# A hybrid layer on one core: attention's first pair of heads built in place beside the values' projection, and the MLP's first pass in a fixed order

## The chip, the cores and the metric

The kernel runs on one core of one Trainium2 chip. The time is the device time of one execution in microseconds (us); lower is better. All times are of float32 inputs of fixed shape (one sequence of 1024 tokens, width 1024).

## What is computed

The reference, cut to what matters here:

```python
h = rms(x) * (1 + scale_m) + shift_m            # scales, shifts, gates: silu(c) @ w_ada + b_ada
proj = h @ w_in                                 # (1024, 4104): fox q,k,v,gate,forget + retention q,k,v,gate
fox = forgetting_attention(rms(fq)*qg, rms(fk)*kg, fv, log_sigmoid(f_logit + b))   # 8 heads of 64
ret = retention(rope(rq), rope(rk), rv)                                            # 4 heads of 128
x = x + gate_m * (concat(rms(fox)*.. , rms(ret)*..) @ w_out)
h = rms(x) * (1 + scale_f) + shift_f
u = square(relu(h @ w_mlp_in))                  # (1024, 4096)
x = x + gate_f * (u @ w_mlp_out)
```

Forgetting attention is causal softmax attention whose logits also take a difference of cumulated forget gates, cum[t] - cum[s].

## The kernel before

**Precision.** Every large product is made of three TensorE matmuls: both operands are split into a rounded part and a remainder (split_w: ScalarE casts, L138, VectorE subtracts, L139), and hi·hi, hi·lo and lo·hi are added up in PSUM. A matmul is 128 rows by 512 columns.

**Stages, in order of time.** Conditioning and norm; the input projections (proj_group, one call for 512 output columns and half the tokens: 8 steps k of 12 matmuls, L295 to L297); the retention chunks, hooked in between; attention over four pairs of heads; the output projection (L937 and after); the second norm; the MLP.

**Attention.** The last projection is that of the values (fv), in two halves. Between them, prep_pair(0) makes the first pair of heads ready: four parts (fk and fq, two halves of the tokens each) transpose four blocks on TensorE (L641), cast and subtract (L644 to L649) into scratch (fkH, part of kl, and for fq the tile wh), and then 11 copies by DMA bring each head's two 64-row halves to the places that the scores want (L656 to L660). Only then is wh free for what it is named for, the cumulated gates of each head over 128 partitions (L662, 512 KB each), because the same tile was the scratch of fq. The second half of fv runs interleaved with the first scores S (L707, L708); VectorE adds the gates and takes the row maximum from PSUM (L711), ScalarE takes exponentials (L723), TensorE transposes p (L743) and multiplies by v (L752). Other pairs are prepared beside the pair ahead of them.

**The MLP's first pass.** It is a Strassen-like scheme in eight "Eighths" e0 to e7, of 512 columns of w_mlp_in each. One Eighth has seven products of 24 matmuls: in order one, two, six, five, seven, three, four. Its weights are four blocks of 512 KB named 11, 21, 12, 22 (load, L1090); products use blocks or differences of them ("tees", L1144 and L1147, 2 = 22 - (12 - 11); six, L1156 and L1157; the difference 2 has a tile named wt). Before a product its block is split (halve) into one of two shared buffers (mr), so the split of one product can run while the one before it multiplies, and no earlier. Results are squared (L1115 to L1118) and u is written to HBM (put, L1122). For e0 and e1 the first products stand in a block written by hand (manual_schedule: TensorE, ScalarE and VectorE follow the program's order), in which the last four token blocks of the second norm are transposed (h2_turn) and combined (make_s2) between the products.

**The gates of the MLP.** w_mlp_out is multiplied by gate_f on GpSimd before the second pass: 32 blocks n, each loaded (gate_load, 512 KB), multiplied in two halves and, for every other pair, subtracted (gate_times, L1201 and L1203), and stored (gate_store, two of 256 KB). There are two buffers. They are hung on the steps of the first pass (52 steps: ten of e0 and e1, then seven per Eighth): n is loaded at step 2 + 3·(n // 2) + n % 2, so two per three steps.

**The MLP's second pass.** Four quarters of seven products of 48 matmuls (L1304) over blocks a.. (of u) and b.., t1 (of the gated weights) that are loaded from HBM (L1275); the first difference on GpSimd is wdt = b22 - t1 (t_two, L1330).

**What sets the order.** A scheduler orders each engine's instructions from a simulated timeline, except in blocks written by hand and for single instructions kept in program order (the gates' DMAs). Nearly all DMAs are issued by one engine, SP, in its order, and an issue that waits holds up those behind it.

The split, and the loop by which the sides are hung on the steps before:

```python
    for n in range(32):
        at = 2 + n // 2 * 3 + n % 2
        for d, what in ((0, gate_load), (1, gate_times), (2, gate_store)):
            side[at + d].append(lambda what=what, n=n: what(n))
```

Of the kernel before, what the change touches and what calls it, by code (L numbers as in the profile page):

```python
# [19 lines left out]
P = 128  # L20
S = 1024
# [28 lines left out]
def tile_block(  # L50
# [573 lines left out]
    def prep_pair(pr):  # L624
# [6 lines left out]
        def part(name, half):  # L631
# [6 lines left out]
            hd, rest = split[name]  # L638
            tp = (xbank if pr else rbank)(f"{name}p{pr}{half}")
            for i in range(4):  # L640
# [24 lines left out]

    proj_group("fv", 2 * FW, 0, evac_fox("fv"), ret_hook(1))
    while todo:
        ada_hook(0)
    for n, m in enumerate((2, 5)):
# [4 lines left out]
        Q.dma_start(rows_d[n, :].rearrange("(k p) -> k p", p=P), gs)  # L674
    for _ in ret:
        pass
    ops, parts = prep_pair(0)
    for part in parts:
# [295 lines left out]
    def h2_norm(t):  # L974

        xt = x2_tok(t)
        rr = r_x[:, t : t + 1]
        A.activation(ra([P, D], f"x2sq{t}"), xt, AF.Square, accum_out=rr)
        V.tensor_scalar(rr, rr, 1.0 / D, EPS, op0=ALU.mult, op1=ALU.add)
        rsqrt_(rr, 1)  # L980
        xn = [t2([P, CH], f"xn{t}{n}") for n in range(2)] if t < 5 else None
# [89 lines left out]
    W2 = 2 * P  # L1071

    class Eighth:
        def __init__(self, e):
# [4 lines left out]
        def load(self, names):  # L1079
            for name, make in (("11", raw), ("21", f4), ("12", f4), ("22", f4)):  # L1080
                if name in names:
                    r, c_ = int(name[0]) - 1, int(name[1]) - 1
                    if self.e == 1 and name == "22":
                        both = s8([P, 2, 4, W2], "wu1_22")
                        self.b["2"], w = both[:, 0], both[:, 1]
# [4 lines left out]
                    Q.dma_start(w, wup_v[:, 4 * r : 4 * r + 4, at : at + W2])  # L1090

        def halve(self, name):
            s = self.split[name] = mr([P, 2, 4, W2], f"wu{self.e}s{name}", F32R)
            split_w(self.b[name], s[:, 0], s[:, 1])

# [24 lines left out]
        def put(self, n, st):  # L1120
            at = self.e % 2 * 2 * CH
            Q.dma_start(u_d[self.e // 2][n][:, at : at + 2 * CH], st.rearrange("p f c -> p (f c)"))  # L1122

# [8 lines left out]
        def two(self):  # L1132
            Y = [self.make[2 + f](f"Y{self.e}_{f}") for f in range(2)]
            self.product("A12", "21", Y, True)
            if self.e > 1:
                self.tees()
            for f in range(2):
                V.tensor_tensor(self.c11[:, f], Y[f], self.c11[:, f], op=ALU.add)
                self.square(self.c11, f)
            self.put(0, self.c11)  # L1140

        def tees(self):
            b = self.b
            V.tensor_tensor(b["12"], b["12"], b["11"], op=ALU.subtract)  # L1144
            if self.e != 1:
                b["2"] = ra([P, 4, W2], f"wt{self.e}")
            V.tensor_tensor(b["2"], b["22"], b["12"], op=ALU.subtract)  # L1147

        def six(self):
# [5 lines left out]
            b = self.b  # L1155
            V.tensor_tensor(b["11"], b["2"], b["11"], op=ALU.subtract)  # L1156
            V.tensor_tensor(b["21"], b["21"], b["2"], op=ALU.subtract)  # L1157

# [31 lines left out]
    def gate_load(n):  # L1190
        if not gf:
            for hf in range(2):
                gf.append(r2([P, CH], f"gf{hf}"))
                Q.dma_start(gf[hf], rows_d[1, hf * CH : (hf + 1) * CH].partition_broadcast(P))
            wg.append(s8([P, 2, 2, CH], "wg"))
        tc.keep_in_program_order(Q.dma_start(wg[0][:, n % 2].rearrange("p h c -> p (h c)"), wdn_v[:, n, :]))

    def gate_times(n):
        w = wg[0][:, n % 2]
        for hf in range(2):  # L1200
            G.tensor_tensor(w[:, hf], w[:, hf], gf[hf], op=ALU.mult)  # L1201
        if n % 4 < 2:
            G.tensor_tensor(w[:, 1], w[:, 1], w[:, 0], op=ALU.subtract)  # L1203

    def gate_store(n):
        e, c_, f = n // 4, n // 2 % 2, n % 2
        at = (e % 2 * 2 + f) * CH
        for hf in range(2):
            tc.keep_in_program_order(Q.dma_start(wd_d[e // 2][2 * c_ + hf][:, at : at + CH], wg[0][:, n % 2, hf]))

# [28 lines left out]
    with tc.manual_schedule(engines={ENG.PE, ENG.Activation, ENG.DVE}):  # L1239
        for n, t in enumerate(HI):  # L1240
            if n == 0:
                e0.one()
            elif n == 1:
                e0.two()
            else:
                e1.one()
            h2_turn(t, xn[t])
            make_s2(t)
            if n == 0:
                e0.tees()  # L1250
# [13 lines left out]
    for what in sum(side[len(steps) :], []):  # L1264
        what()

    x2b = []
    for q in range(4):
# [46 lines left out]

        for name in ("a11", "b11", "a12", "b21"):
            load(name)
        X = [lower[i](f"V{q}_{i}") for i in range(4)]
        product(1, blk["a11"], two("b11"), X, True, 0)
        if q == 0:  # L1320
            for n in range(4):
                x2b.append(s8([P, 2, D], f"x2b{n}"))
                Q.dma_start(x2b[n].rearrange("p i d -> p (i d)"), x2_d[n])
        for name in ("s1", "t1", "b22"):
            load(name)
        add(X, 0, 0)
        V.tensor_tensor(blk["a11"], blk["s1"], blk["a11"], op=ALU.subtract)  # L1327
        t_two = [raw([P, 2, CH], f"wdt{q}{g}") for g in range(2)]
        for g in range(2):
            G.tensor_tensor(t_two[g], two("b22")(g), two("t1")(g), op=ALU.subtract)  # L1330
# [6 lines left out]
        load("a22")  # L1337
        product(6, blk["a11"], lambda g: t_two[g], X, False, 0)
        add(X, 0, 1)
# [59 lines left out]
```

## Time and profile before

| what | value |
|---|---|
| three runs | 1384.39, 1377.92, 1380.03 us, median 1380.03 |
| the profiled execution | 1383.38 us, of which the span of the trace is 1381.6 |
| granted TensorE clock, mean of the span | 0.975 |
| TensorE busy | 1288.2 us, 93% of the span |
| VectorE, ScalarE, GpSimd busy | 974.7, 515.8, 460.4 us |

Times in the trace count from the start of its span. The table of engines says how long each had an instruction in flight; it doesn't say who waited for whom. In a timeline a row has start, length, engine, line, operation, the written and the read tiles, the shape, how many are put together (x24), and in brackets the idle time before it and what ended it.

### The profile page before, as it was taken

How to read it: one execution, taken by the hardware profiler on the slowest of the kernel's cores; microseconds unless marked ns; L12 is line 12 of the kernel's file. 1: busy time of each engine (PE TensorE's matmuls, PEld its weight loads, DVE VectorE, ACT ScalarE, POOL GpSimd, SP SyncE). 2: the span in 40 equal slices, each digit the busy share in tenths (PEclk: the TensorE clock that was granted, in tenths of full speed). 3: DMA queues.
4: the chain of work that ended last, by engine and by line, in shares of the span. 5: the costliest groups of instructions: out<-in, count | busy, mean ns of one | idle time of the engine just before them, and what ended most of it. 6: DMA issues, size and time to landing. Idle time of an engine off the chain costs nothing. (4 is left out here: it accounts for less than half of the span.)

```text
span 1381.6 us, 16679 instructions
## 1 busy us (share of the span) xinstructions
PE 1288.2 (93%) x6131; PEld 1042.5 (75%) x6131; DVE 974.7 (71%) x1486; ACT 515.8 (37%) x801; POOL 460.4 (33%) x364
## 2 busy tenths in 40 slices
PE   5899899999999899999976898889999899999998
PEld 3678777888888666678864786678888778888887
DVE  6758897476754367753687574668867989888883
ACT  3642212343333366652544432222334242424240
POOL 1129451156622013322340034644553714050500
PEclk9899999999999999999997999999999999999999
DMA  9656566534357574832550348667669450514202
GB/s 292 187 126 164 151 171 141 132 100 139 115 168 174 140 166 116 291 138 78 181 168 16 107 160 263 218 221 234 234 208 354 179 215 29 199 46 152 92 31 92
DMA packets 123601, 220.51 MB, mean 160 GB/s; under 512 B 9896, under 2 KB 70376, under 8 KB 117888
## 3 DMA queue, kind: packets, MB, share of 16 engines
q1 hardware_dynamic: 100640, 202.68, 47.8%
q10 hardware_dynamic: 22880, 16.78, 3.9%
q8 instruction: 48, 0.79, 0.2%
q14 instruction: 33, 0.27, 0.1%
HBM read 159.55 MB, written 48.34 MB: 150 GB/s over the span
## 5 line engine op out<-in xcount | busy, mean ns | idle before, releaser
L1304 PE MATMUL V<-sb,sa 128*128 128x512 f32 x768 | 180.3, 392 | 6.0 <-DVE sb L139 4.7
L1201 POOL TENSOR_TENSOR wg<-wg,gf 128x512 f32<-128x512 f32 x64 | 107.5, 1703 | 223.1 <-DMA wg<-in_w_mlp_out_dram 120.0
L1304 PEld LDWEIGHTS V<-sb,sa 128*128 128x128 f32 x768 | 145.1, 189 | 37.8 <-DVE sb L139 5.9
L135 POOL TENSOR_TENSOR sm<-sm 128x8 f32<-128x8 f32 (+2 forms) x48 | 62.0, 1298 | 138.5 <-DVE sm L253 48.8
L1304 PE MATMUL U<-sb,sa 128*128 128x512 f32 x384 | 88.8, 389 | 0.0
L1304 PEld LDWEIGHTS U<-sb,sa 128*128 128x128 f32 x384 | 72.1, 188 | 14.9
L138 ACT CAST sb<-b 128x1024 fp32r<-128x1024 f32 x40 | 40.7, 1052 | 103.5 <-PE V L1304 57.5
L238 DVE SCALAR_TENSOR_TENSOR wa<-wa,sm 128x128 f32<-128x128 f32 (+1 forms) x154 | 72.4, 470 | 3.3
L1330 POOL TENSOR_TENSOR wdt<-b,t 128x1024 f32<-128x1024 f32 x8 | 24.3, 3060 | 136.9 <-DMA b<-wd_d 136.9
L1282 DVE TENSOR_TENSOR x2b<-V,x2b 128x512 f32<-128x512 f32 x64 | 42.5, 683 | 35.0 <-PE V L1304 35.0
L711 DVE CUSTOM_DVE_ANT_0 p<-S,wh 128x512 f32<-128x512 f32 (+3 forms) x96 | 49.9, 552 | 24.1 <-DMA wh<-nc_d 16.2
L139 DVE TENSOR_TENSOR sa<-a,sa 128x2048 fp32r<-128x2048 f32 x20 | 60.3, 3015 | 4.2 <-ACT sa L138 4.1
L139 DVE TENSOR_TENSOR sb<-b,sb 128x1024 fp32r<-128x1024 f32 x40 | 55.4, 1410 | 3.5 <-ACT sb L138 1.6
L701 POOL TENSOR_SCALAR_AFFINE_SELECT wh<-wh 128x128 f32<-128x128 f32 x64 | 18.2, 293 | 108.2 <-DVE sm L711 53.1
L723 ACT ACTIVATE p<-p,sm 128x1024 f32<-128x1024 f32 (+7 forms) x64 | 49.1, 770 | 4.4 <-DVE sm L719 3.7
L707 PE MATMUL S<-kt,qt 128*128 128x512 f32 (+3 forms) x96 | 38.7, 408 | 9.2 <-DVE sm L711 6.6
L138 ACT CAST sa<-a 128x2048 fp32r<-128x2048 f32 x20 | 38.2, 1911 | 22.3 <-DVE a L1327 11.0
L1304 PE MATMUL W<-sb,sa 128*128 128x512 f32 x192 | 45.1, 389 | 0.0
L743 PE MATMUL pt<-ident,p 128*128 128x128 f32 x288 | 40.6, 282 | 2.6 <-ACT p L723 2.6
L743 PEld LDWEIGHTS pt<-ident,p 128*128 128x128 f32 x288 | 31.7, 142 | 13.4 <-issue 8.1
L1304 PEld LDWEIGHTS W<-sb,sa 128*128 128x128 f32 x192 | 36.1, 188 | 7.5
L752 PE MATMUL av<-pT,fv 128*64 128x256 f32 (+1 forms) x320 | 40.2, 373 | 0.0
(391 smaller groups left out, 3449.3 us busy)
## 6 DMA issues: line engine op xcount, KB each, us to landing
wu<-in_w_mlp_in_dram SPq DMA_DIRECT2D x32, 512.0 KB, 4.5
wg<-in_w_mlp_out_dram SPq DMA_DIRECT2D x32, 512.0 KB, 4.8
wd_d<-wg SPq DMA_DIRECT2D x64, 256.0 KB, 3.6
a<-u_d SPq DMA_DIRECT2D x12, 1024.0 KB, 6.4
b<-wd_d SPq DMA_DIRECT2D x12, 1024.0 KB, 7.1
wa<-in_w_ada_dram ACTq DMA_DIRECT2D x10, 1024.0 KB, 5.7
wam<-in_w_ada_dram SPq DMA_DIRECT2D x16, 512.0 KB, 7.7
u_d<-ua SPq DMA_DIRECT2D x16, 512.0 KB, 3.0
```

Of the source, the lines that this page charges most:

```text
L135: G.tensor_tensor(ap, ap, mhalf.to_broadcast([P, n]), op=ALU.pow)
L138: A.copy(h_ap, raw_ap)
L139: eng.tensor_tensor(l_ap, raw_ap, f32(h_ap), op=ALU.subtract)
L238: V.scalar_tensor_tensor(w[:, 0], w[:, j], c_act[:, j : j + 1], w[:, 0], op0=ALU.mult, op1=ALU.add)
L707: T.matmul(sp[n], qt[:, n, dg], kt[:, n, c_], start=True, stop=False)
L711: V.tensor_tensor_reduce(ps[n][:, c_], sp[n], wh[:, n, c_], -1.0, 3.4e38, op0=ALU.add, op1=ALU.min, accum_out=mcs[n][c0 // CH])
L723: A.activation(ps[n][:, :W], ps[n][:, :W], AF.Exp, bias=mcs[n][0], scale=-1.0, accum_out=den[:, 2 * i + n : 2 * i + n + 1],)
L743: T.transpose(tp[:, n, i * P : (i + 1) * P], ps[i][n][:, j * P : (j + 1) * P], ident)
L752: T.matmul(av[own, at], fox_pair_of("fv", pr)[:, j, n * FD : (n + 1) * FD], pts[j][:, n, i0 * P :], start=(j == 0), stop=(j == 2 * gg + 1),)
L1201: G.tensor_tensor(w[:, hf], w[:, hf], gf[hf], op=ALU.mult)
L1282: V.tensor_tensor(xs, banks[i], xs, op=ALU.add)
L1304: T.matmul(banks[i], sa[pa][:, a, ii], sb[pb_][a // 2][:, a % 2, :], start=(first and a == 0 and m == 0), stop=(a == 3 and m == 2), skip_g ...
```

## The change

1. **Attention.** The first pair gets a function of its own, first_pair. ScalarE and VectorE write each head's own 64 partitions straight into kt, kl and qt, two operations of 64 partitions where one of 128 stood (four more on each of the two engines), the remainder of q goes to a tile of its own (fqL), the two loads of the gates go out first, and 6 copies by DMA are left of 11. The four parts are called at k = 2, 4, 6 of the first half of fv and right after it.
2. **The second norm** of five token blocks uses other buffers (r2 for t2), which leaves t2 to the gates' gf.
3. **The hand-written block.** e1's block 11 is split right behind e0's tees, e1's 21 ahead of e1's first product, e0's difference 2 behind e1's second product; adding and squaring c11 of e0 and e1 leaves the block. e1's 22 and 2 become two half tiles each.
4. **The first pass.** SP follows the program's order through all steps. Stores of u go out one step later, behind that step's sides. The gates have four buffers and are loaded at step 12 + n, one per step, each in two DMAs.
5. **The second pass.** The first loads are a11, b11, t1, b22, a12, b21; t_two comes ahead of the first product; of the four x2b loads two stand behind product 1 and two behind a22.

The core of the diff:

```diff
+    def first_pair(pr):
+        klt, kt, qt, wh = (s8([P, 2, S], f"{name}{pr}", dt) for name, dt in (("kl", F32R), ("kt", F32R), ("qt", F32R), ("wh", F32)))
+        for n in range(2):
+            Q.dma_start(wh[:, n, :], nc_d[2 * pr + n, :].partition_broadcast(P))
...
+            if name == "fk":
+                for n, (own, _) in enumerate(ROWS):
+                    A.copy(kt[own, n, hs], tp[own, :])
+                for n, (own, _) in enumerate(ROWS):
+                    V.tensor_tensor(klt[own, n, hs], tp[own, :], f32(kt[own, n, hs]), op=ALU.subtract)
...
+    def prep_hook(k):
+        ada_hook(k)
+        if k == 0:
+            ops, made = first_pair(0)
+            parts.extend(made)
+        elif k % 2 == 0:
+            parts.pop(0)()
-    proj_group("fv", 2 * FW, 0, evac_fox("fv"), ret_hook(1))
+    proj_group("fv", 2 * FW, 0, evac_fox("fv"), prep_hook)
...
-        at = 2 + n // 2 * 3 + n % 2
+        at = 12 + n
...
+        e0.one()
+        h2_turn(HI[0], xn[HI[0]])
+        make_s2(HI[0])
+        e0.tees()
+        e1.halve("11")
+        e0.two()
+        h2_turn(HI[1], xn[HI[1]])
+        make_s2(HI[1])
+        e1.halve("21")
+        e1.one()
+        h2_turn(HI[2], xn[HI[2]])
+        make_s2(HI[2])
         e1.two()
+        e0.halve("2")
     e1.tees()
+    e0.end_two()
     split_part("S1", "r21", whole)
+    e1.end_two()
...
-    for n, step in enumerate(steps):
-        step()
-        for what in side[n]:
+    with tc.manual_schedule(engines={ENG.SP}):
+        for n, step in enumerate(steps):
+            due = list(stores)
+            stores.clear()
+            step()
+            for what in side[n] + due:
...
-        for name in ("a11", "b11", "a12", "b21"):
+        for name in ("a11", "b11", "t1", "b22", "a12", "b21"):
             load(name)
```

**What moves on TensorE, in the second half of fv.** Before, the first scores come behind the fifth step (ws_fv_4):

```order
L297 MATMUL pp_fv_3669<-ws_fv_4_3766,hT_355 128x512
L295 MATMUL pp_fv_3673<-ws_fv_4_3766,hT_355 128x512
L296 MATMUL pp_fv_3673<-ws_fv_4_3766,hT_355 128x512
L297 MATMUL pp_fv_3673<-ws_fv_4_3766,hT_355 128x512
L707 MATMUL S_3683<-kt_3602,qt_3603 128x512
L708 MATMUL S_3683<-kl_3601,qt_3603 128x512
L295 MATMUL pp_fv_3661<-ws_fv_5_3793,hT_397 128x512
```

and with the change inside the third step (ws_fv_2) of the last token block, two heads close together:

```order
L296 MATMUL pp_fv_3676<-ws_fv_1_3694,hT_223 128x512
L297 MATMUL pp_fv_3676<-ws_fv_1_3694,hT_223 128x512
L295 MATMUL pp_fv_3676<-ws_fv_2_3723,hT_269 128x512
L757 MATMUL S_3686<-kt_3434,qt_3435 128x512
L758 MATMUL S_3686<-kl_3433,qt_3435 128x512
L296 MATMUL pp_fv_3676<-ws_fv_2_3723,hT_269 128x512
L757 MATMUL S_3687<-kt_3434,qt_3435 128x512
L758 MATMUL S_3687<-kl_3433,qt_3435 128x512
```

The six score tiles of 512 columns (two matmuls each) now all stand inside the second half; before, the last two came behind its last matmul. Three of the four groups of transposes (L641, now L676) moved from the second half of fv into the first.

**What moves on ScalarE, in the hand-written block.** ua is the tile of c11 and c22, h2S that of the combined second-norm rows, wu1s that of e1's split. Before, the cast of e1's 11 stands behind the third h2S cast:

```order
L1115 ACTIVATE ua_6358<-ua_6358 128x512
L1116 ACTIVATE ua_6358<-ua_6358 128x512
L1004 ACTIVATE h2r_6089<-h2p_6419,sm 128x128 x4
L1012 CAST h2S_6106<-h2r_5904 128x4x128
L138 CAST wu1s_6443<-wu_11_6297 128x1024
L1130 COPY ua_6470<-X_0_6441 128x512
```

and with the change behind the second, ahead of the next transposed rows (h2p):

```order
L1054 ACTIVATE h2r_6092<-h2p_6366,sm 128x128 x4
L1186 ACTIVATE ua_6363<-ua_6363 128x512
L1187 ACTIVATE ua_6363<-ua_6363 128x512
L1062 CAST h2S_6109<-h2r_5907 128x4x128
L138 CAST wu1s_6391<-wu_11_6300 128x1024
L1054 ACTIVATE h2r_6092<-h2p_6420,sm 128x128 x4
```

The squaring of c11's first half (L1186, L1187) still stands ahead of it.

**What moves on SP, in e2.** wg is a gate block, wd_d where it is stored, wu3_22 the block 22 of e3. Before, gates, stores of u and loads stand as the scheduler put them:

```order
L1196 DMA wg_6651<-in_w_mlp_out_dram 128x1024 x2
L1122 DMA u_d10_89<-ua2_6947 128x1024
L1209 DMA wd_d02_103<-wg_6651 128x512
L1090 DMA wu3_22_7106<-in_w_mlp_in_dram 128x4x256
L1209 DMA wd_d03_104<-wg_6651 128x512
```

and with the change the step "seven" stores one gate block, loads another and then loads wu3_22:

```order
L1193 DMA u_d10_89<-ua2_6930 128x1024
L1273 DMA wg_7012<-in_w_mlp_out_dram 128x512 x2
L1286 DMA wd_d00_101<-wg_7012 128x512
L1286 DMA wd_d01_102<-wg_7012 128x512
L1273 DMA wg00_7013<-in_w_mlp_out_dram 128x512
L1273 DMA wg01_7014<-in_w_mlp_out_dram 128x512
L1154 DMA wu3_22_7094<-in_w_mlp_in_dram 128x4x256
```

The three loads 11, 21, 12 of an Eighth now stand at the step "one" of the Eighth ahead of it. VectorE's order of the splits and differences of e2 to e7 is the same in both kernels: the difference 2 of the next Eighth stands ahead of the split of 22 for the product three.

## Rows read from the trace of the kernel before

**Rows 1.** Stretches: bounds, length, busy time (instructions) of PE, PEld, DVE, ACT, POOL; clock, DMA, GB/s.
```profile
441.50:476.40 34.90, 29.57 (x130) 22.03 (x128) 12.91 (x36) 11.44 (x21) 1.75 (x6) 1.00 0.73 168
...
705.40:814.90 109.50, 87.61 (x361) 68.66 (x362) 73.89 (x88) 47.74 (x70) 9.15 (x7) 0.91 0.28 92
814.90:1064.30 249.40, 234.79 (x1010) 192.66 (x1009) 178.69 (x163) 74.38 (x95) 127.72 (x76) 0.97 0.71 240
1064.30:1117.50 53.20, 47.29 (x198) 37.75 (x196) 48.60 (x33) 21.61 (x16) 28.34 (x10) 0.97 0.53 209
1117.50:1377.90 260.40, 260.32 (x1147) 215.28 (x1147) 209.22 (x175) 82.09 (x64) 60.76 (x18) 1.00 0.28 104
```

**Rows 2.** Timeline of TensorE, around the second half of fv and the first scores.
```profile
460.02 0.47 PE L707 MATMUL S<-kt,qt 128*128 128x512 f32 x1 [1.48 <-issue]
...
476.40 0.44 PE L743 MATMUL pt<-ident,p 128*128 128x128 f32 x2 [2.01 <-ACT p L723]
...
478.62 0.78 PE L707 MATMUL S<-kt,qt 128*128 128x512 f32 x1
```

**Rows 3.** Timeline of VectorE: the first row maximum.
```profile
466.06 0.69 DVE L711 CUSTOM_DVE_ANT_0 p<-S,wh 128x512 f32<-128x512 f32 x1 [8.40 <-DMA wh<-nc_d]
```

**Rows 4.** Timeline of TensorE in the products of e0 and e1.
```profile
714.60 5.74 PE L1103 MATMUL Y<-h2A,wu0s 128*128 128x512 f32 x24
...
730.97 8.63 PE L1103 MATMUL X<-h2A,wu1s 128*128 128x512 f32 x24 [9.76 <-ACT wu1s L138]
...
746.13 1.22 PE L1103 MATMUL Y<-h2A,wu1s 128*128 128x512 f32 x2 [5.66 <-ACT wu1s L138]
...
761.26 5.60 PE L1103 MATMUL X<-h2S,wu1s 128*128 128x512 f32 x24
766.70 5.60 PE L1103 MATMUL Z<-h2S,wu0s 128*128 128x512 f32 x24
```

**Rows 5.** Timeline of VectorE: a difference of 128x1024 that waits for a load, GpSimd idle.
```profile
779.32 1.23 DVE L1144 TENSOR_TENSOR wu<-wu,wu 128x1024 f32<-128x1024 f32 x1 [4.19 <-DMA wu<-in_w_mlp_in_dram]
```

**Rows 6.** Timeline of SP in e0 and e1; the length is that of both DMAs, waits included.
```profile
726.38 38.10 SPq L1122 DMA_DIRECT2D u_d<-ua  x2
```

**Rows 7.** Timeline of TensorE in e2 to e4: its stalls, and the product behind the last.
```profile
843.72 7.43 PE L1103 MATMUL X<-h2S,wu2s 128*128 128x512 f32 x20 [6.02 <-DVE wu2s L139]
...
915.66 7.33 PE L1103 MATMUL Y<-h2A,wu4s 128*128 128x512 f32 x20 [3.81 <-DVE wu4s L139]
922.82 5.61 PE L1103 MATMUL X<-h2S,wu4s 128*128 128x512 f32 x24
```

**Rows 8.** Timeline of VectorE in e2 and e5: the difference 2 of the next Eighth.
```profile
841.31 1.22 DVE L1147 TENSOR_TENSOR wt<-wu,wu 128x1024 f32<-128x1024 f32 x1 [11.05 <-DMA wu<-in_w_mlp_in_dram]
...
971.50 2.29 DVE L1147 TENSOR_TENSOR wt<-wu,wu 128x1024 f32<-128x1024 f32 x1 [2.16 <-DMA wu<-in_w_mlp_in_dram]
973.71 2.31 DVE L139 TENSOR_TENSOR wu5s<-wu,wu5s 128x1024 fp32r<-128x1024 f32 x1
```

**Rows 9.** Timeline of GpSimd: multiplications beside VectorE's work, and with VectorE idle.
```profile
817.46 8.32 POOL L1201 TENSOR_TENSOR wg<-wg,gf 128x512 f32<-128x512 f32 x4 [101.40 <-DVE ub L1183]
...
833.73 2.53 POOL L1201 TENSOR_TENSOR wg<-wg,gf 128x512 f32<-128x512 f32 x2 [4.55 <-DMA wg<-in_w_mlp_out_dram]
```

**Rows 10.** GpSimd's busy time (instructions) of L1201 alone, in two stretches of e2 to e7.
```profile
814.90:922.80 107.90, 45.93 (x28) 0.94 0.69 228
922.80:1064.30 141.50, 54.67 (x32) 1.00 0.73 249
```

**Rows 11.** The page's DMA issues: KB each, us from issue to landing.
```profile
wu<-in_w_mlp_in_dram SPq DMA_DIRECT2D x32, 512.0 KB, 4.5
wg<-in_w_mlp_out_dram SPq DMA_DIRECT2D x32, 512.0 KB, 4.8
```

**Rows 12.** Timeline of TensorE, where the second pass's third product begins.
```profile
1091.49 6.44 PE L1304 MATMUL V<-sb,sa 128*128 128x512 f32 x20 [3.69 <-DVE sb L139]
```

**Rows 13.** Timeline of GpSimd at the begin of the second pass.
```profile
1079.98 7.08 POOL L1330 TENSOR_TENSOR wdt<-b,t 128x1024 f32<-128x1024 f32 x2 [5.59 <-DMA b<-wd_d]
```

More of the change, by code (lines that the diff above doesn't have):

```diff
@@ L664, in prep_pair, with part @@
         return (klt, kt, qt, wh), [lambda name=name, half=half: part(name, half) for name in ("fk", "fq") for half in (1, 0)]
[L666 removed]
+    def first_pair(pr):
+        klt, kt, qt, wh = (s8([P, 2, S], f"{name}{pr}", dt) for name, dt in (("kl", F32R), ("kt", F32R), ("qt", F32R), ("wh", F32)))
+        rests = []
+        for n in range(2):
+            Q.dma_start(wh[:, n, :], nc_d[2 * pr + n, :].partition_broadcast(P))
+        def part(name, half):
+            tp = rbank(f"{name}p{pr}{half}")
+            for i in range(4):
+                T.transpose(tp[:, i * P : (i + 1) * P], fox_pair_of(name, pr)[:, half * 4 + i, :], ident)
+            hs = slice(half * CH, (half + 1) * CH)
+            if name == "fk":
[3 more added lines that the diff above has]
+                    V.tensor_tensor(klt[own, n, hs], tp[own, :], f32(kt[own, n, hs]), op=ALU.subtract)
+            else:
+                if half:
+                    rests.append(ra([P, S], f"fqL{pr}", F32R))
+                for n, (own, _) in enumerate(ROWS):
+                    A.activation(qt[own, n, hs], tp[own, :], AF.Identity, scale=qkg[own, :])
+                for n, (own, _) in enumerate(ROWS):
+                    V.scalar_tensor_tensor(
+                        rests[0][own, hs], tp[own, :], qkg[own, :], f32(qt[own, n, hs]), op0=ALU.mult, op1=ALU.subtract
+                    )
+            if half:
+                return
+            for n, (own, oth) in enumerate(ROWS):
+                if name == "fk":
+                    for t in (kt, klt):
+                        Q.dma_start(f32(t[oth, n, :]), f32(t[own, n, :]))
+                else:
+                    Q.dma_start(f32(qt[oth, n, :]), f32(rests[0][own, :]))
+        return (klt, kt, qt, wh), [lambda name=name, half=half: part(name, half) for name in ("fk", "fq") for half in (1, 0)]
+    for _ in ret:
+        pass
+    parts = []
+    def prep_hook(k):
+        nonlocal ops
+        ada_hook(k)
[4 more added lines that the diff above has]
+            parts.pop(0)()
+    ops = None
+    proj_group("fv", 2 * FW, 0, evac_fox("fv"), prep_hook)
     while todo:
@@ L980, in h2_norm @@
         rsqrt_(rr, 1)
-        xn = [t2([P, CH], f"xn{t}{n}") for n in range(2)] if t < 5 else None
+        xn = [r2([P, CH], f"xn{t}{n}") for n in range(2)] if t < 5 else None
         if xn is None:
@@ L1071, in tile_block, with pieces, minus @@
     W2 = 2 * P
+    stores = []
+    def pieces(w):
+        return w if isinstance(w, list) else [w]
+    def minus(dst, u, v):
+        if any(isinstance(w, list) for w in (dst, u, v)):
+            dst, u, v = (w if isinstance(w, list) else [w[:, 0:2], w[:, 2:4]] for w in (dst, u, v))
+        for a, b, c_ in zip(pieces(dst), pieces(u), pieces(v)):
+            V.tensor_tensor(a, b, c_, op=ALU.subtract)
     class Eighth:
@@ L1083, in load @@
                     if self.e == 1 and name == "22":
-                        both = s8([P, 2, 4, W2], "wu1_22")
-                        self.b["2"], w = both[:, 0], both[:, 1]
+                        w = self.halves(name)
                     else:
@@ L1259, in tile_block @@
     split_part("S4", "r12", whole)
-    for n, step in enumerate(steps):
-        step()
-        for what in side[n]:
+    with tc.manual_schedule(engines={ENG.SP}):
[4 more added lines that the diff above has]
+            for what in side[n] + due:
+                what()
+        for what in sum(side[len(steps) :], []) + stores:
             what()
-    for what in sum(side[len(steps) :], []):
-        what()
     x2b = []
@@ L1314, in two, with load_x2 @@
             return lambda g: blk[name][:, 2 * g : 2 * g + 2]
-        for name in ("a11", "b11", "a12", "b21"):
+        for name in ("a11", "b11", "t1", "b22", "a12", "b21"):
             load(name)
+        def load_x2(n):
+            x2b.append(s8([P, 2, D], f"x2b{n}"))
+            Q.dma_start(x2b[n].rearrange("p i d -> p (i d)"), x2_d[n])
+        t_two = [raw([P, 2, CH], f"wdt{q}{g}") for g in range(2)]
+        for g in range(2):
+            G.tensor_tensor(t_two[g], two("b22")(g), two("t1")(g), op=ALU.subtract)
         X = [lower[i](f"V{q}_{i}") for i in range(4)]
@@ L1320, in tile_block @@
         if q == 0:
[L1321 to L1325, printed above, removed]
+            load_x2(0)
+            load_x2(1)
+        load("s1")
         add(X, 0, 0)
         V.tensor_tensor(blk["a11"], blk["s1"], blk["a11"], op=ALU.subtract)
-        t_two = [raw([P, 2, CH], f"wdt{q}{g}") for g in range(2)]
-        for g in range(2):
-            G.tensor_tensor(t_two[g], two("b22")(g), two("t1")(g), op=ALU.subtract)
         Y = [upper[i](f"W{q}_{i}") for i in range(4)]
```

63 lines of the change are left out of this document (32 added, 31 removed).

## The prediction

> **What bounds the kernel now.** I read the waits of TensorE first, then the stretches between them. TensorE is the engine at which the time is lost or kept: from 1117.5 to 1377.9 it is busy for 260.32 of 260.40 us [rows 1], so a gain there is not to be had. The loss stands in four places ahead of it, and each has its own cause:
>
> - The second half of fv, 441.5 to 476.4: 34.90 - 29.57 = 5.33 us idle [rows 1]. The first score waits 1.48 us for copies of q [rows 2], VectorE waits 8.40 us for the gates in wh [rows 3], and the first transposed p waits 2.01 us for its exponential [rows 2].
> - The products of e0 and e1. A product takes 766.70 - 761.26 = 5.44 us [rows 4]. From 714.60 to 814.9 there are 13 products, 70.7 us, and three groups of transposes of some 0.5 us that are not overlapped: 72.3. The stretch is 100.3 long, so 28.0 are lost: waits of 9.76 and 5.66 us are among them [rows 4], and matmuls at a granted clock of half speed (the 24 that start at 730.97 take 8.63 us, where others take 5.60).
> - e2 to e7, 814.9 to 1064.3: 42 products are 228.5 us, the stretch is 249.4, 21 lost. All of it lies ahead of 922.82: from there to 1064.3 stand exactly 26 products of 5.44 us [rows 1, 7]. The two longest stalls are 6.02 and 3.81 us, and after each the clock falls to half (20 matmuls take 7.43 and 7.33 us, where 24 take 5.61) [rows 7]. Behind them are loads that come late: wt waited 11.05 us for its block [rows 8], just ahead of the first.
> - The first products of the second pass, where one waits 3.69 us [rows 12] and, by the difference of 53.20 and 47.29 [rows 1], 5.9 us are idle; with the matmuls at half clock behind that wait and a few short gaps I put this place at 9.
>
> **Attention.** The same TensorE work is done; what can go is idle time. With the transposes in the first half of fv, and the copies and gates on their way before the second half starts, I take away the waits of the scores and of the first row maximum, 5.33 - 2.01 = 3.3 us. The 2.01 us stays: behind the last score stand a row maximum, a small operation and an exponential, whatever came earlier. The score that starts at 478.62 takes 0.78 us where 0.47 stands at 460.02 [rows 2]: the clock was at half speed after these gaps, and without most of them I count 1.5 us for that. Added: four small operations each on ScalarE and VectorE, and four copies ahead of two weight loads on SP. They lie in the first half of fv, where both engines wait for loads. If that cover were gone, eight operations at 0.69 us (the length of a 512-column one [rows 3]) would cost 5.5. So **4.8 us gained**, between a loss of 0.7 and a gain of 7.
>
> **e0 and e1.** I follow the new order from 714.60, with the lengths of before. VectorE does a difference of e1, the rows of the next block, the two halves of difference 2, c11's first half and the combination by 721.0; ScalarE then casts h2S and e1's 11 by 722.7; VectorE has h2S, two differences of e0 at 1.22 and then the split of 11 ready at 725.9. The product needs that at its third matmul, so it ends at about 730.9, where before it started at 730.97 and ended at 739.4 [rows 4]. The split of 21 comes behind four differences and a combination on VectorE (735.3), so the second product ends at 740.3. Difference 2 of e0 is split behind the last combination, one subtraction of 2048 columns, one remainder of 2048 and c11's add: 746.6. The product six of e0 then ends at 751.6, and up to 2.5 later if the clock falls in the gap before it. Before, that point is 761.26: **8.5 us gained**, between 7 and 10. The rest, 761.26 to 814.9, is nine products, 49.0 us, and 4.7 lost, because e2's loads stood on SP behind stores of u that took 38.10 us [rows 6], and VectorE waited 4.19 us for one of them with the splits queued behind [rows 5]. In the new order c11 is squared some 10 us earlier and the loads go out behind it: I take 3.5 of the 4.7. Together **12 us gained**, between 7 and 14.7.
>
> **e2 to e7.** Two things act. The late loads go: 11, 21 and 12 are issued a whole Eighth ahead. Block 22 of the next Eighth is issued at "seven", behind a gate block that was loaded two steps earlier: it lands in 4.8 us [rows 11] and is multiplied in two or three operations, at 1.27 us each with VectorE idle and at 8.32/4 = 2.08 beside its work [rows 9]. I put the issue at 20 to 22 us after the Eighth's start, the landing 4.5 later [rows 11], at 24.5 to 26.5. VectorE needs it for wt, ahead of the split for three, which starts at 27.2. In e5, whose first product starts 27.2 before the three at 977.2, wt began 21.5 in, at 971.50, and wt and the split, at 2.3 each, were just in time [rows 8]. So five times a stall of 0 to 3 us; I take 1.5, 7.5 in all. The second thing is GpSimd: 80 operations (64 multiplications, 16 subtractions) in 32 steps, 2.5 a step. Before, the 26 steps without a stall had 32 multiplications [rows 10] and 8 subtractions, 1.5 a step; the 18 or so ahead of them 28 and 8, 2 a step, with the stalls. VectorE's 1.23 [rows 5] becomes 2.3 when GpSimd works [rows 8]: one operation of the other fits between. I take 5.5 us of stalls for this. In sum 13 of the 21 remain: **8 us gained**; the ends are 21 (no stall, as from 922.82 on) and 0 or a loss of 5.
>
> That 1.23 becomes 2.3 is what the trace shows; that it always must, it doesn't. The Trainium skill ("SBUF — State Buffer", Who interferes with whom) has it as a rule, and it speaks against this change: a VectorE instruction with two SBUF inputs and a GpSimd one that reads SBUF shut each other out for the whole instruction. By the rows my sum is 28.3; by a strict rule it would be 20.3, which is the first rival below.
>
> **The second pass.** t_two (7.08 us, from 1079.98 [rows 13]) now runs ahead of the first product, as its blocks are loaded third and fourth; the wait of 3.69 us [rows 12] and the half clock behind it, some 2, come from it. What remains is the split of that product, behind the adds of the second. **3.5 us gained**, between 0 and 7. If GpSimd is late from the gates, nothing is gained; but its last gates now end seven steps before.
>
> **Sum.** 4.8 + 12 + 8 + 3.5 = 28.3. The profiled execution took 1383.38 us (span 1381.6), 3.35 above the median of the runs, 1380.03. 1383.4 - 28.3 = 1355.1; against the median, **1352**.
>
> **Rivals.**
>
> - *Contention takes back e2 to e7.* Every two-input operation of VectorE waits for one of GpSimd. Counting an Eighth's: 11 of 1024 columns at 1.23 and 8 of 512 at 0.69, 19 us, over 32 steps (32/7 Eighths) 87; GpSimd 80 at 1.27, 102; in series 189 us, and 32 products are 174. 15 us lost, and with 6 for block 22 the whole 21: time 1360. For it: 2.5 operations a step are more than the trace has anywhere; against it: GpSimd may lag without holding TensorE up. By the rule of the Trainium skill ("SBUF — State Buffer", Who interferes with whom) the series is strict.
> - *No stall is left in e2 to e7*, and e0 and e1 give 14: 1352 - 13 - 2 = 1337. For it: 141 us without a stall at 1.5 operations a step.
> - *Little comes of it*: moved waits reappear at the next product (six of e0 behind VectorE, the exponential in attention): 1370 to 1378, with half of e0 and e1's gain and none elsewhere 1374.
> - *The gates pace TensorE, and it is slower.* SP now keeps one order, so a late gate holds block 22 up. Two gate blocks cost 5 operations; at 2.08 that is 10.4 us, and 4.8 for landing makes 15.2 if the next two loads wait for both. The pace of the products is 10.88 per two steps: 16 times 4.3 is 69 us of stalls in place of 21, a loss of 48, less 20.3 from the other places: 1380 + 28 = 1408. It decides from 16 × (c - 10.88) = 21 + 20.3, c = 13.5 us for two blocks. Against it: four buffers, so the loads overlap the multiplications.
>
> **Chances.** Forecast 0.56, contention 0.20, no stall 0.09, little 0.09, gates 0.06. The range holds the first three and part of the fourth: the lower end is the case without a stall with attention at its upper end, the upper that of contention with e0 and e1 at 7 and the second pass at nothing, 1360 + 5 + 3.5: **1335 to 1368**. A measurement tells 0.5% (6.9 us) from no change: faster is below 1373.1. Faster 0.56 + 0.20 + 0.09 + 0.03 = 0.88, same 0.06, slower 0.06.
>
> **What would show it.** In the profile of the changed kernel: the first pt some 3 us after the last fv matmul and no wait for wh; e1's first product starting 8 us (not 16) after the second product of e0 began, though it waits again at its third matmul; the second pass beginning 25 us earlier, about 1039; stalls of three in e2 to e6 waiting for wu..s splits with wt behind a load; GpSimd busy over 4 us of each 5.44 in the 32 steps. If the first pass has stalls over 21 us, or SP waits for gates while wu loads queue behind, the third term was wrong; if a wait of over 5 us stands before six of e0, the second.

## The result and the profile after

The changed kernel takes 1358.69 us (median of three, 1357.97 to 1361.46) where the kernel before takes 1380.03: a ratio of 0.984, with an interval of 0.982 to 0.987. It is faster by 21.3 us. The prediction was 1352, 1335 to 1368.

So that two traces can be compared whose starts differ by a few us, I cut them at the same instructions: the first matmul of fv, the first transposed p (pt), the product two of e0, the product one of e2, the first matmul of the second pass, the end. The stretches are differences of those starts.

| stretch, us | before | after | gained | predicted |
|---|---|---|---|---|
| start to fv | 418.6 | 419.6 | -1.0 | 0 |
| fv to pt | 57.8 | 52.6 | 5.2 | 4.8 |
| pt to e0's two | 238.2 | 239.4 | -1.2 | 0 |
| e0's two to e2 | 100.3 | 84.9 | 15.3 | 12 |
| e2 to e7 | 249.4 | 251.9 | -2.5 | 8 |
| second pass to the end | 317.3 | 311.2 | 6.1 | 3.5 |
| span | 1381.6 | 1359.7 | 21.9 | 28.3 |

Three terms came out larger than predicted. The one of e2 to e7 gained nothing: 2.5 us are lost in this execution, and some 1 us is gained in runs e2 and e3 below, which have the same first pass. The first and third stretch say nothing by differences of this size: between the executions below they vary from 418.6 to 426.1 and from 233.7 to 242.5 us. The stretches of the changed kernel, in the columns of [rows 1] and next to its lines:

```profile
437.40:472.30 34.90, 32.43 (x151) 26.64 (x149) 16.66 (x42) 14.24 (x26) 1.17 (x4) 1.00 0.44 117
711.70:796.60 84.90, 78.47 (x330) 63.37 (x329) 65.31 (x79) 43.01 (x62) 0.73 (x1) 0.93 0.21 73
796.60:1048.50 251.90, 237.90 (x1009) 194.61 (x1008) 174.03 (x160) 77.28 (x96) 136.02 (x82) 0.96 0.76 260
1048.50:1101.70 53.20, 51.42 (x224) 41.59 (x223) 52.19 (x42) 18.65 (x15) 12.78 (x5) 1.00 0.46 180
1101.70:1356.00 254.30, 254.30 (x1123) 210.25 (x1121) 195.01 (x167) 81.74 (x64) 58.04 (x18) 1.00 0.25 96
```

Ahead of the first pt 2.47 us are idle where 5.33 were; the first 53 us of the second pass have 1.8 idle where 5.9 were; e2 to e7 have 14.0 idle, as much as before (14.6), and a clock of 0.96. The timeline of TensorE in e2 to e7 shows where. These four rows, all of the product three (Z), are its only stalls:

```profile
864.97 6.45 PE L1174 MATMUL Z<-h2S,wu3s 128*128 128x512 f32 x20 [1.99 <-DVE wu3s L139]
...
909.61 6.84 PE L1174 MATMUL Z<-h2S,wu4s 128*128 128x512 f32 x20 [4.63 <-DVE wu4s L139]
...
955.57 7.70 PE L1174 MATMUL Z<-h2S,wu5s 128*128 128x512 f32 x20 [5.59 <-DVE wu5s L139]
...
998.73 6.44 PE L1174 MATMUL Z<-h2S,wu6s 128*128 128x512 f32 x20 [1.78 <-DVE wu6s L139]
```

Before, one stall stood at seven of e2 (6.02 us), two stood at two and three of e3, one at two of e4 (3.81 us) [rows 7], and e5 to e7 had none. The two of e3 in the trace of before:

```profile
869.97 4.85 PE L1103 MATMUL Y<-h2A,wu3s 128*128 128x512 f32 x20 [1.59 <-DVE wu3s L139]
...
895.24 4.83 PE L1103 MATMUL Z<-h2S,wu3s 128*128 128x512 f32 x20 [3.19 <-DVE wu3s L139]
```

Now one stands in each of e3 to e6, always at the product three. From the start of a three to that of the four behind it these four take 9.35, 12.38, 14.19 and 9.13 us, where 5.44 would do: 23.3 us more, within 0.1 us all that the stretch is above 42 products without a gap (251.9 - 228.5). Of these, 14.0 are idle; the other 9.3 are matmuls at a lower granted clock (20 of them take 6.44 to 7.70 us, where 24 take 5.60; the clock from 902.0 to 916.3 is 0.76). The rows that lead to the second of them, SP first (u_d<-ua is the store of c11, wd_d a gate block's, wu the load of e5's block 22), then VectorE:

```profile
891.44 0.33 SPq L1193 DMA_DIRECT2D u_d<-ua  x1
891.86 3.28 SPq L1286 DMA_DIRECT2D wd_d<-wg  x2
895.20 0.92 SPq L1273 DMA_DIRECT2D wg<-in_w_mlp_out_dram  x2
896.22 2.42 SPq L1286 DMA_DIRECT2D wd_d<-wg  x2
898.68 0.90 SPq L1273 DMA_DIRECT2D wg<-in_w_mlp_out_dram  x2
899.68 0.41 SPq L1154 DMA_DIRECT2D wu<-in_w_mlp_in_dram  x1
```

```profile
906.12 1.23 DVE L1134 TENSOR_TENSOR wt<-wu,wu 128x1024 f32<-128x1024 f32 x1 [8.99 <-DMA wu<-in_w_mlp_in_dram]
907.27 2.28 DVE L139 TENSOR_TENSOR wu4s<-wu,wu4s 128x1024 fp32r<-128x1024 f32 x1
```

e4's first product starts at 876.71. The load goes out 23.0 us later, behind the store of c11 and the stores and loads of two gate blocks; SP stands 3.28 and 2.42 us at the two gate stores, waits included. It lands 6.4 us after that; VectorE stands 8.99 us idle ahead of wt; and the split that the product three needs is queued behind wt. The issues of e3, e5 and e6 come 20.6, 24.2 and 22.0 us after their Eighth's start; that of e2, 17.2 us after it, cost nothing.

### The profile page after: what moved, and what is told of

Its sections match the earlier page's. It is cut to its first block, busy times and chain, and to the rows that moved or that the text cites. A ratio compares the mean times of both kernels' runs of the same rounds, so it can differ in the third digit from the quotient of the medians.

```text
span 1359.7 us, 16691 instructions
## 1 busy us (share of the span) xinstructions
PE 1282.2 (94%) x6131; PEld 1040.6 (77%) x6131; DVE 962.9 (71%) x1495; ACT 519.2 (38%) x807; POOL 450.1 (33%) x364
## 4 chain that ended last, share of the span: by engine, by line
PE 37%; DVE 6%; DMA 6%; POOL 5%; issue 2%; SPq 1%; ACT 1%; DVEq 0%; POOLq 0%; ACTq 0%
PE V L1388 12%; PE U L1388 6%; PE X L1174 6%; PE Z L1174 4%; DMA wg<-in_w_mlp_out_dram 4%; POOL wg L1278 3%; PE W L1388 2%; DMA wu<-in_w_mlp_in_dram 2%; PE Y L1174 1%; PE po_woA L1000 1%; PE po_woA L999 1%; PE po_woA L1001 1%; POOL wg L1280 1%; POOL x L1006 1%; DVE sb L139 1%
## 5 line engine op out<-in xcount | busy, mean ns | idle before, releaser
L1278 POOL TENSOR_TENSOR wg<-wg,gf 128x512 f32<-128x512 f32 x64 | 103.8, 1642 | 157.5 <-DMA wg<-in_w_mlp_out_dram 157.5
L1388 PEld LDWEIGHTS U<-sb,sa 128*128 128x128 f32 x384 | 72.1, 188 | 14.9
L1409 POOL TENSOR_TENSOR wdt<-b,t 128x1024 f32<-128x1024 f32 x8 | 19.4, 2452 | 146.8 <-DMA b<-wd_d 109.7
L139 DVE TENSOR_TENSOR sa<-a,sa 128x2048 fp32r<-128x2048 f32 x20 | 52.4, 2622 | 8.1 <-PE V L1388 5.6
L138 ACT CAST sa<-a 128x2048 fp32r<-128x2048 f32 x20 | 38.1, 1910 | 32.2 <-DVE a L1417 15.9
L1423 POOL TENSOR_TENSOR b<-b,wdt 128x1024 f32<-128x1024 f32 x8 | 27.3, 3415 | 49.0 <-DVE sb L139 49.0
```

The costliest lines, as they stand in the source:

```text
L138: A.copy(h_ap, raw_ap)
L139: eng.tensor_tensor(l_ap, raw_ap, f32(h_ap), op=ALU.subtract)
L1278: G.tensor_tensor(w[hf], w[hf], gf[hf], op=ALU.mult)
L1388: T.matmul(banks[i], sa[pa][:, a, ii], sb[pb_][a // 2][:, a % 2, :], start=(first and a == 0 and m == 0), stop=(a == 3 and m == 2), skip_g ...
```

## The experiments

A run is written with the word run (run e4); e0 to e7 alone are Eighths, as in "e2 to e7". Stretches in us, cut as above, in each run's profiled execution:

| run | two of e0 to e2 | e2 to e7 | second pass | median of the runs |
|---|---|---|---|---|
| before | 100.3 | 249.4 | 317.3 | 1380.03 |
| the change | 84.9 | 251.9 | 311.2 | 1358.69 |
| e1, attention alone | 100.0 | 247.4 | 317.2 | 1377.12 |
| e2, no early splits | 96.2 | 248.6 | 313.1 | 1373.07 |
| e3, old order in the second pass | 85.3 | 248.1 | 311.1 | 1363.32 |
| e4, block 22 first | 85.6 | 233.6 | 312.8 | 1345.66 |
| e5, e3 and late gates | 83.5 | 246.9 | 318.8 | 1366.45 |
| e6, e4 without multiplications | 83.7 | 228.5 | 311.0 | 1338.58 |
| e7, e4 with three gates in four steps | 83.6 | 244.7 | 315.2 | 1356.91 |
| e8, stores two steps later | 85.7 | 239.0 | 311.5 | 1350.58 |
| e9, the change and late gates | 85.0 | 252.0 | 314.9 | one run, 1370.38 |
| e10, e4 and e8 and all loads first | 84.0 | 239.6 | 311.0 | 1351.09 |
| e11, e4, c11 squared on ScalarE | 84.4 | 235.3 | 312.9 | 1348.78 |

The stretch from fv to pt is 52.6 in every run with the new attention. Runs e2 and e3 have the changed first pass as it is, and e5 and e9 have it with the last four gate blocks later; they give e2 to e7 at 246.9 to 252.0, so differences of 5 us there say nothing. The medians are of whole executions and hold the scatter of the stretches that a run didn't change: differences of a few us between them aren't read either.

**Run e1.** The kernel before with first_pair and its hook, nothing else.

```diff
-    proj_group("fv", 2 * FW, 0, evac_fox("fv"), ret_hook(1))
...
+    proj_group("fv", 2 * FW, 0, evac_fox("fv"), prep_hook)
...
-    ops, parts = prep_pair(0)
```

> The kernel before with the attention part of the change alone. Theory (what the changed kernel's trace suggests): the first transposed p starts some 4 us earlier than at 476.40, and about as much is left at the end, 2.5 to 4.5 us (ratio 0.997 to 0.998). Rival: the gain is absorbed behind attention, because the output projection waits for loads; then the span is that of before within 1 us although the first transposed p is early.

The stretch from fv to pt is the 52.6 of the change, and the three behind it (100.0, 247.4, 317.2) are those of before or within 2 us of it. The ratio is 0.999 (0.9976 to 1.0003): 5.2 us are gained at pt, but this execution reached fv 3.7 us later, and the kernel's time resolves no better. The gain is shown in the trace, and by the times alone it isn't.

**Run e2.** The change without its three early splits.

```diff
-        e1.halve("11")
...
-        e1.halve("21")
...
-        e0.halve("2")
```

> The changed kernel without the three early splits in the hand-written block (e1's 11 and 21, e0's difference 2 are split where their products stand). Theory: the early splits carry 8.8 of the 15.3 us that the stretch from e0's second product to e2's first one got shorter, so that stretch goes from 85 to 92 to 95 us; the rest comes from e2's loads going out early. Rival: the fixed order of SP carries all of it, and the stretch stays within 2 us of 85.

96.2 us, outside the range of the theory too: the early splits carry 11.3 of the 15.3, more than I had said. The two waits of before are back, within 0.4 us of their lengths in [rows 4]:

```profile
730.13 8.64 PE L1174 MATMUL X<-h2A,wu1s 128*128 128x512 f32 x24 [9.37 <-ACT wu1s L138]
...
745.30 1.22 PE L1174 MATMUL Y<-h2A,wu1s 128*128 128x512 f32 x2 [5.65 <-ACT wu1s L138]
...
760.42 5.60 PE L1174 MATMUL X<-h2S,wu1s 128*128 128x512 f32 x24
```

From 760.42 to e2's first product at 809.38 stand nine products of 5.44 without a gap, where before 4.7 us were lost. That part came with the rest of the change; I put it down to the order of SP, which no run moves by itself.

**Run e3.** The change with the second pass in its old order: a11, b11, a12, b21 first; t1 and b22 behind product 1; t_two behind them; four x2b loads in a row.

> The changed kernel with the loads, t_two and the x2b loads of the second pass in the order of before. Theory: the 6.2 us that the second pass got shorter come from t_two ahead of the first product (311.2 us from its first matmul to the end of the span goes back to 314 to 317). Rival: they come from the gates having ended before it begins; then it stays at 311 to 312.

311.1, within 0.1 us of what the change has: the rival holds. The new order of loads and t_two gives nothing here. (The median is 4.6 us above the change's; none of that lies in the second pass of this trace.)

**Run e4.** One move on SP: block 22's load goes ahead of its step's gates.

```diff
-        side[at].append(lambda e=e: eighths[e].load(("22",)))
+        side[at].insert(0, lambda e=e: eighths[e].load(("22",)))
```

> The changed kernel with one move: at the step seven, the load of block 22 of the next Eighth goes ahead of the gate block's store and load on SP. GpSimd does the same work at the same rate. Theory (late load): the load goes out 3 to 4 us earlier, and the four stalls of the product three, 23.3 us of lost time together, shrink to 3 to 10 us; the kernel is 13 to 20 us faster than the change. Rival (contention between GpSimd and VectorE): the stalls stay within 4 us of 23.3.

233.6: 18.3 of the 23.3 us are gone (14.5 against run e3, the lowest of the others with the loads and gates of the change), with GpSimd's 82 operations in the stretch as before. The kernel is at 0.976 (0.974 to 0.977) of the kernel before, and the fastest of those that compute the whole layer; by the medians it is 13.0 us faster than the change. In the Eighth e4 the load goes out at 893.73, 20.5 us after the Eighth's start (23.0 in the change), in the Eighth e3 17.3 after it (20.6), and the product three of e4 goes through without a stall:

```profile
893.73 0.38 SPq L1154 DMA_DIRECT2D wu<-in_w_mlp_in_dram  x1
```

```profile
901.50 5.62 PE L1174 MATMUL Z<-h2S,wu4s 128*128 128x512 f32 x24
...
921.58 4.83 PE L1174 MATMUL Y<-h2A,wu5s 128*128 128x512 f32 x20 [2.33 <-DVE wu5s L139]
```

The longest stall left is the last row. VectorE is not waiting for a load just ahead of it: from 899.5 to 921.6 it works without a break, mostly at 2.2 to 2.3 us for a split or difference that takes 1.22 when GpSimd rests (run e6). But the first row of that stretch is a wt that had waited 4.84 us for block 22:

```profile
899.49 1.57 DVE L1134 TENSOR_TENSOR wt<-wu,wu 128x1024 f32<-128x1024 f32 x1 [4.84 <-DMA wu<-in_w_mlp_in_dram]
...
911.15 2.31 DVE L139 TENSOR_TENSOR wu5s<-wu,wu5s 128x1024 fp32r<-128x1024 f32 x1
913.49 2.21 DVE L1134 TENSOR_TENSOR wu<-wt,wu 128x1024 f32<-128x1024 f32 x1
...
919.24 2.28 DVE L139 TENSOR_TENSOR wu5s<-wu,wu5s 128x1024 fp32r<-128x1024 f32 x1
```

This wt starts 26.2 us after the start of e4, where in run e6 it starts 22.5 after it. So the load may still have a part in what is left.

**Runs e5 and e9.** The last four gate blocks eight steps later, with the second pass in its old order (e5, built on e3) and in its new one (e9).

```diff
-        at = 12 + n
+        at = 12 + n + (8 if n >= 28 else 0)
```

> The kernel of e3 (the changed kernel with the second pass's loads and t_two in the order of before), with the last four gate blocks eight steps later, so that they end about where they ended before. Theory (the gates' early end is what the second pass gained): from 311.2 us, the stretch from the second pass's first matmul to the end goes to 314 to 319. Rival (the fixed order of SP and the deferred stores gave it): it stays within 1.5 us of 311.2.

> The changed kernel, second pass in its own new order, with the last four gate blocks eight steps later, as in e5. Theory: t_two ahead of the first product doesn't help by itself (e3) and waits for the late gates on GpSimd and SP all the same, so the stretch from the second pass's first matmul to the end is 315 to 321 us, as e5's 318.9. Rival: the new order shields the first products from late gates, and it stays within 2 us of 311.2.

Run e5: 318.8, 7.7 more than run e3. The gates' early end is what the second pass gained. GpSimd's multiplications stand ahead of t_two again, as in the trace of before (first row, ahead of [rows 13]; the other two are of run e5):

```profile
1067.49 6.90 POOL L1201 TENSOR_TENSOR wg<-wg,gf 128x512 f32<-128x512 f32 x4 [20.85 <-DMA wg<-in_w_mlp_out_dram]
```

```profile
1055.11 4.60 POOL L1278 TENSOR_TENSOR wg<-wg,gf 128x512 f32<-128x512 f32 x2 [14.40 <-DMA wg<-in_w_mlp_out_dram]
1060.81 7.73 POOL L1418 TENSOR_TENSOR wdt<-b,t 128x1024 f32<-128x1024 f32 x2 [1.10 <-DMA b<-wd_d]
```

A product behind them waits for a split of VectorE, which works beside GpSimd there:

```profile
1074.06 6.27 PE L1388 MATMUL U<-sb,sa 128*128 128x512 f32 x15 [3.41 <-DVE sa L139]
```

Run e9: 314.9, 0.1 below the theory's range and 1.7 above the rival's. With late gates the new order saves 3.9 of the 7.7, by one execution each; with gates that end in time it saves nothing (run e3). In both runs the late gates' stores also stand on SP ahead of loads of the second pass, so which of SP and GpSimd carries the 7.7 isn't separated.

**Run e6.** e4 without gate_times (gate_f and the differences of w_mlp_out's blocks are left out).

> The kernel of e4 (block 22 first) without the multiplications and subtractions of the gates on GpSimd: the blocks of w_mlp_out are loaded and stored as they are, so gate_f and the differences of its blocks are left out. Theory (what is left of the loss in e2 to e7, 5.1 us, is contention between GpSimd and VectorE): the stretch goes from 233.6 to 228.5 to 229.5 us. Rival (it is late loads still): it stays above 231.

228.5, which is 42 products of 5.44, without an idle moment:

```profile
796.10:1024.60 228.50, 228.50 (x1010) 189.27 (x1009) 145.40 (x160) 77.38 (x96) 5.21 (x2) 1.00 0.82 287
```

VectorE's 160 instructions take 145.4 us, where in run e4 the same 160 take 185.9 beside GpSimd's 144. So the last 5.1 us belong to the multiplications. Without them SP waits for no multiplication either, and block 22's load goes out earlier (16.5 us after the start of e4, not 20.5). The rows of run e4 show both, slower VectorE and a late load; which of them carries the 5.1 us isn't separated.

**Run e7.** e4 with the gates spread over more steps, 1.9 operations of GpSimd per step in place of 2.5.

```diff
-        at = 12 + n
+        at = 6 + n * 4 // 3
```

> The kernel of e4 with the gate blocks hung on steps 6 to 47, three per four steps, in place of one per step on steps 12 to 43. Theory: with GpSimd's 2.5 operations per step down to 1.9 the stalls that e4 left in e2 to e7 shrink from 5.1 us to 1 to 3; e0 and e1 and the second pass stay as they are; the kernel is 1 to 4 us faster than e4. Rival: gates in the steps of e0 and e1 delay its splits and loads, and what e2 to e7 win is lost there.

A miss, and on no side foreseen: e0 and e1 lost nothing (83.6), e2 to e7 got worse by 11 us (244.7), all of it in e2 to e4 and in e7, and the second pass by 2.5 (315.2 against 312.8), with gates that end four steps later. The place of one stall shows a reason. SP stands 4.26 us at a gate's store, and the load of block 22 behind it goes out 35.3 us after the start of e2, where in run e4 it is 14.9 (in e3 33.6 and 17.3). wt waits 4.33 us for that load, and what is queued behind it is now the split for the next Eighth's one, for which TensorE stands 2.15 us:

```profile
828.44 4.26 SPq L1286 DMA_DIRECT2D wd_d<-wg  x2
832.79 0.39 SPq L1154 DMA_DIRECT2D wu<-in_w_mlp_in_dram  x1
```

```profile
837.22 1.22 DVE L1134 TENSOR_TENSOR wt<-wu,wu 128x1024 f32<-128x1024 f32 x1 [4.33 <-DMA wu<-in_w_mlp_in_dram]
838.37 0.68 DVE L1249 TENSOR_TENSOR ub<-Z,ub 128x512 f32<-128x512 f32 x1
838.97 1.21 DVE L139 TENSOR_TENSOR wu3s<-wu,wu3s 128x1024 fp32r<-128x1024 f32 x1
```

What the rate alone would give stays open.

**Run e8.** The change, with the stores of u one step later still; block 22 stays behind the gates.

```diff
+            due = late[:]
+            late[:] = stores
```

> The changed kernel with the stores of u issued two steps after their product in place of one; block 22 stays behind the gate block of its step. It tells what holds block 22 up on SP. Theory A (the store of c11, for which SP waits at the step six): the stretch e2 to e7 falls from 251.9 to 235 to 243 us. Theory B (the gate block's store and load): it stays above 246.

239.0, in theory A's range: waiting for c11's squares held block 22 up too, and taking that away saves 12.9 us of the stretch (8.1 by the medians). The load goes out 20.0 to 21.8 us after the start of e3 to e6, where it was 20.6 to 24.2. The stalls of three are gone but for 0.23 us; new ones of 1.02 to 2.29 us stand at two of e3 to e6. At the two longest VectorE waits for a load, 1.34 and 2.44 us ahead of the next Eighth's 12 - 11, with the split of 21 queued behind; at the other two it works without a break.

**Run e10.** e4, e8, and every load of w_mlp_in first in its step.

> e4 and e8 together, and the loads of 11, 21 and 12 ahead of the gate block of their step too: every load of w_mlp_in goes out first in its step, stores of u two steps after their product. Theory: what is left in e2 to e7 is contention alone, so the stretch is 230 to 234 us, no more than 3 us better than e4's 233.6. Rival: e8's new stalls at the product two (1.0 to 2.3 us) stay, and it is 235 or more.

239.6, worse than run e4 by 6.0: on the rival's side by the number, but of its place only one stall of two is left (1.56 us); the others stand at seven, but for 0.42 us at six. The difference wt now stands ahead of the split for seven on VectorE, and waits there for its load:

```profile
898.45 1.23 DVE L1134 TENSOR_TENSOR wt<-wu,wu 128x1024 f32<-128x1024 f32 x1 [6.11 <-DMA wu<-in_w_mlp_in_dram]
899.59 1.22 DVE L139 TENSOR_TENSOR wu4s<-wu,wu4s 128x1024 fp32r<-128x1024 f32 x1
```

```profile
900.86 6.43 PE L1174 MATMUL X<-h2S,wu4s 128*128 128x512 f32 x20 [2.73 <-DVE wu4s L139]
```

With the load earlier in the program the scheduler here put the difference that reads it earlier on VectorE too; the load doesn't come as early as that (it goes out 19.8 us after the start of e4, 20.5 in run e4), and the stall moves to the product ahead.

**Run e11.** e4 with c11 of every Eighth squared on ScalarE.

```diff
-            if self.e < 2 and st is not self.c12:
+            if st is not self.c12 if self.e < 2 else st is self.c11:
```

> e4 with the squaring of c11 in e2 to e7 as two operations on ScalarE in place of one on VectorE (two operations of 512 columns less per Eighth that read only SBUF). Theory (what is left of the loss is VectorE held up by GpSimd): the stretch e2 to e7 goes from 233.6 to 230 to 232.5 us. Rival: ScalarE's casts of the splits are held up by the added 2.5 us per Eighth, and it becomes 234 or more.

235.3, a miss of the theory: VectorE is busy for 170.6 us in place of 185.9, ScalarE for 90.7 in place of 77.3, and the stretch is no shorter than run e4's. Two short operations less per Eighth don't matter here: the longest stall stands where it stood, at two of e5 (2.18 us, 2.33 in run e4), and waits for VectorE's split. The number is on the rival's side; that ScalarE's casts are what holds it there isn't shown.

## Why the prediction held, and where it failed

That the time fell into the range is in part luck. Three terms came out 0.4, 3.3 and 2.6 us larger than predicted, and these 6.3 us cover most of the 10.5 by which e2 to e7 fell short.

- **Attention, 4.8 predicted, 5.2 measured.** The waits for copies and for wh are gone, and the last one stays, 2.47 us where I had said 2.01. But the 1.5 us for the clock didn't come: the first score behind pt still takes 0.77 us, as at [rows 2]. In their place 2.3 us came that I hadn't counted. TensorE's idle time from fv to pt fell by 2.86; the rest I put down to the breaks in the stream that are gone. The first matmul of each of the six 512-column scores took 457 ns in the mean and now takes 389, which is 0.4 us in sum; the remainder isn't shown.
- **Between pt and e0's two, 0 predicted, 1.2 lost.** e0's first product came 1.3 us earlier in its stretch, but the next block's rows waited for the norm as before (3.57 us in place of 2.66). The scatter of this stretch, 233.7 to 242.5 us, is larger than the loss.
- **e0 and e1, 12 predicted, 15.3 measured.** The steps came at the places that I had worked out:

```profile
711.68 7.71 PE L1174 MATMUL Y<-h2A,wu0s 128*128 128x512 f32 x24
...
720.43 0.73 PE L1174 MATMUL X<-h2A,wu1s 128*128 128x512 f32 x2 [0.17 <-ACT wu1s L138]
724.31 7.75 PE L1174 MATMUL X<-h2A,wu1s 128*128 128x512 f32 x22 [3.14 <-DVE wu1s L139]
...
734.35 5.74 PE L1174 MATMUL Y<-h2A,wu1s 128*128 128x512 f32 x24 [1.43 <-ACT h2r L1054]
...
743.91 4.83 PE L1174 MATMUL X<-h2S,wu0s 128*128 128x512 f32 x20 [0.20 <-DVE wu0s L139]
```

  e1's first product starts 8.75 us after e0's two (8 predicted) and waits at its third matmul; its remainder comes 12.6 in (11.3 predicted); six of e0 runs from 32.2 in (32.0 predicted). What I under-sized is the rest. All 4.7 us of the late loads went, not 3.5. Ahead of them 10.7 us are gained and not 8.5: some matmuls of e1's six run inside the gap ahead of e0's, and the clock didn't fall in that gap (20 matmuls in 4.83 us), for which I had allowed up to 2.5.
- **e2 to e7, 8 gained predicted, 2.5 lost.** This is the step that failed, by its size: "five times a stall of 0 to 3 us; I take 1.5". The mechanism and the product were right, and four stalls came. I had 7.5 us for five of them; the four cost 23.3, of which 14.0 are idle (3.5 a stall) and 9.3 are matmuls at a lower clock behind the stalls, which this term had put at nothing. I had put the issue at 20 to 22 us and the landing 4.5 later; the issue came at 20.6 to 24.2 and the landing 5.4 to 6.4 later (the trace tells three of the five). The 4.5 is the page's median over the whole kernel [rows 11]; for the loads of e2 to e7 alone the trace of before already had 5.3, by the six landings that it tells. What comes later than wt is needed goes on to TensorE. The prediction's own sign for this is in the rows above: SP waits for gates while a wu load stands behind them. For contention I had 5.5 us; run e6 bounds the multiplications' whole part in run e4 at 5.1, with a load in it that goes out later than run e6's, and in the change itself it isn't separated.
- **The second pass, 3.5 predicted, 6.1 measured, for another reason.** I had t_two's place in the order carry it. Run e3 shows that place to be worth nothing here, and run e5 that the gates' end is worth 7.7, on GpSimd and SP together. The clause "its last gates now end seven steps before" was the term, and I had it as a condition.
- **The rivals.** By the time, the first rival's 1360 was nearer than my 1352 (1.3 and 6.7 us off), but its mechanism isn't the main part of what happened: run e4 takes back 18.3 of the 23.3 us without touching GpSimd's work. The Trainium skill's rule on VectorE and GpSimd ("SBUF — State Buffer", Who interferes with whom) fits the lengths of 2.2 to 2.3 us in run e4's rows, where 1.22 stands with GpSimd idle, and VectorE's 40 us more beside GpSimd (run e4 against e6). The rival had 15 us for contention in this stretch, and run e6 bounds it at 5.1 once the load is moved; VectorE is busy for 185.9 of the 233.6 us there. Of the slower rival, SP holding block 22 up behind gates, the place was right; moving the load gave 18 us of the stretch, where the rival had 69.

## What to carry to other kernels

In a fixed order of a DMA queue, ask of every load what stands ahead of it and what that waits for: here one 512 KB load stood behind two gate blocks and a store, and one place further up gave 18 us of its stretch and 13 us of kernel time. Price a landing by the stretch it falls in, not by a median of the whole kernel, and a stall with the slower matmuls behind it. When an instruction that waits for a load moves, look at what is queued behind it on its engine: in run e10 the stall came back at another product. When other traffic of the queue moves, look at the load again: in run e7 the gates moved, and the load stood behind them once more.

## What the runs showed that I had not expected

The granted clock fell behind shorter gaps than in the trace of before. There 20 matmuls behind a wait of 3.19 us took 4.83 us (895.24, above), and the clock from 890.9 to 899.9 is 1.00, the upper of its two levels (2.4 GHz). In the changed kernel 20 behind a wait of 1.99 us took 6.45, and the stretch from 861.9 to 871.3 shows 0.82. In run e4 the same number behind 2.33 us took 4.83. So in these runs the length of the last gap doesn't decide by itself: a wait of some 2 us cost 1.6 us more or nothing.

```profile
861.90:871.30 9.40, 7.41 (x26) 5.59 (x25) 8.77 (x9) 1.05 (x1) 5.86 (x3) 0.82 0.35 129
```
